# Seven steps instead of one ahead of a group of transposes, their copies on VectorE, and an output block in other PSUM banks

## The chip, the cores and the metric

The kernel runs on one core of a Trainium2 chip. The metric is the device time of one launch in microseconds (us). TensorE (PE in the profile) multiplies matrices out of SBUF into the banks of PSUM; VectorE (DVE), ScalarE (ACT) and GpSimd (POOL) work on SBUF and PSUM; SyncE (SP) issues the transfers. Each engine runs its own instructions in order and waits on semaphores for the others. A difference of 0.2% is 3.05 us here.

## The reference, cut to what matters

One layer of a diffusion backbone: 1024 latent and 256 context tokens of width 1024, all in fp32. One input projection feeds two groups of heads, a gated DeltaNet in chunks of 64 tokens and a neighbourhood attention; one output projection takes both back to the residual stream.

```python
def gated_deltanet(p, ...):                # p = modulate(rms_norm(x)) @ w_in
    qkv = short_conv(p[..., :3 * DN_WIDTH], conv_w)
    ...
    q = l2_normalize(q) * DN_HEAD_DIM ** -0.5
    k = l2_normalize(k)
    ...
def chunk_gated_delta_rule(q, k, v, g, beta, S0):
    m = jnp.where(strict, einsum("bhncd,bhnmd->bhncm", kb, k) * decay, 0.0)
    a_mat = jnp.eye(CHUNK) + m
    u = triangular_solve(a_mat, v * beta, lower=True, unit_diagonal=True)
    w = triangular_solve(a_mat, kb * exp(gam), lower=True, unit_diagonal=True)
    ...
x = x + g1 * (concatenate([dn_x, na_x], axis=-1) @ w_out)      # the output projection
x = x + g2 * swiglu(modulate(rms_norm(x, norm2_w), sh2, sc2), w_ffn_in, w_ffn_out)
```

The kernel solves the triangular systems by inverses: it inverts 32x32 diagonal blocks of `a_mat` and builds the rest of each chunk's inverse from them by matmuls.

## The kernel before, in words

**Matmuls.** A product of fp32 accuracy is made of three: each operand is split into a high part and a rest (`whi`, `wlo` of the weights, `hh`, `hl` of the activations) and PE sums `hh`*`whi`, `hl`*`whi` and `hh`*`wlo`. For each block of 128 weight columns SP loads `wraw` (line 216), ACT casts it to `whi` (217), and POOL or DVE makes `wlo` (219). `wraw`, `whi` and `wlo` have two buffers each.

**The projection stage.** `jobs` is a list of blocks of output columns. A Block of 1024 tokens is 48 matmuls: 8 steps of the contraction, k, with 3 products into 2 PSUM banks (`blk`). The order that matters here is `nk3` (a wide one of 1280 tokens), `nq0`, `nq1`, `nq2`, `q0`, `q1`, `q2`, `q3`. After a block ACT takes its banks out (line 463, `cacc<-blk`); one block later its norm is made: PE sums squares with matmuls `m<-cr,cst` and `pr<-cr,cst`, ACT reads those banks (line 521), DVE scales (528, 534) and so on. The banks named `m` are two, and are shared by everything that asks for a small bank: the norms and the transposes below.

**Work between the matmuls.** Two generators, `block_inverses()` and then `preps()`, are queued as background work `bg`. After each step k of a block the loop does `bg.step(1)` (for blocks ahead of `turn`, thus up to `q0`), which runs the generator to its next `yield`; what it emits there lands at this place of every engine's program. So a `yield` moves everything that follows in the two generators by one step k, six matmuls.

**block_inverses().** `N` holds the 80 groups of 32x32 blocks, one group a partition. DVE eliminates over the columns (lines 914 and 916, from wide to narrow). Then comes a memset of the diagonal (919), and 8 PE transposes each into two `m` banks (`m<-cst,N`, line 925), copied out of each bank to `WK` (927; `U` is a view of `WK`), with a yield after every second bank: four groups of 8 transposes. Then DVE transposes in squares (933), scales (936), and SP stores the halves to `x_d` (935, 938). Line 103 and line 99 of the profile are the helpers through which all transposes and matmuls go.

**preps().** It loads `xc` from `x_d` (965), `kk` and `e`, spreads `xc` into `fx` and `y` (977, 978), multiplies `kk` by `e` on DVE (982), and then PE makes `pr<-fx,kk` and three `pr<-y,kk`, with copies between them (992, 1000). It is done four times before it needs the queries' blocks, up to `q1`.

**The output projection.** Eight blocks b of 128 output channels, 48 matmuls each for b = 2 to 5, into two banks. ACT and DVE take the products out: `add` is one `scalar_tensor_tensor` into `x2` per bank (line 1460), a square on ACT (1465) and an addition to `acc` (1474) on DVE. Blocks 0 and 1 were begun earlier in other banks (`sc`). The scans before had a PSUM pool `psg`, whose tag `ps` has two banks; `scopes.close()` gives it back and the pool `psf` (8 banks) is opened, ahead of block 2. Between, DVE also works on `acc` from `wad` (lines 251 and 253) for the second half of the modulation.

The order of instructions of each engine is that of the program's text, so it is fixed when the kernel is built.

Of the kernel before, what the change touches and what calls it, by code (L numbers as in the profile page):

```python
# [16 lines left out]
PSUM = bass.MemoryType.PSUM  # L17
# [71 lines left out]
def hybrid(ctx, tc, a, dbg):  # L89
    nc = tc.nc  # L90
    act, dve, pool, sp = nc.scalar, nc.vector, nc.gpsimd, nc.sync
# [16 lines left out]
    def pools(stack, name, side=None, bufs=1, **kw):  # L108
        if side:
            kw["side"] = side  # L110
        return stack.enter_context(tc.tile_pool(name=name, bufs=bufs, reuse_waits="tile", **kw))
# [111 lines left out]
    def modulation(adp, qs, bank):  # L223

        order = [(q, k) for q in qs for k in range(KT)]
        landing = []

        def fetch():
            if order:
                q, k = order.pop(0)  # L230
                x = adp.tile([128, 512], F32, name="wad", tag="wad", bufs=4)
                sp.dma_start(x, a["wa2"][q, :, k])
                landing.append(x)

        def reduce(q, acc2):
            p = bank()
            for b in range(4):
                pe.matmul(p[:, b:b + 1], acc2[:, b * 128:(b + 1) * 128], ones[:, 0:1], start=True, stop=True)
            s = slice(16 + q * 4, 20 + q * 4)
            dve.tensor_tensor(modp[:, s], p[:, 0:4], bada[:, s], OP.add)  # L240

        for _ in range(3):
            fetch()
        prev = None
        for q in qs:
            acc2 = adp.tile([128, 512], F32, name="acc2", tag="acc2", bufs=2)
            for k in range(KT):
                yield
                x, sc = landing.pop(0), sc2[:, k, 0:1]
                if k == 0:  # L250
                    dve.tensor_scalar(acc2, x, sc, None, op0=OP.mult)
                else:
                    dve.scalar_tensor_tensor(acc2, x, sc, acc2, op0=OP.mult, op1=OP.add)  # L253
                fetch()
                if k == 7 and prev is not None:
                    reduce(q - 1, prev)
            prev = acc2
        for _ in range(6):
            yield
        reduce(qs[-1], prev)  # L260
# [133 lines left out]
    with ExitStack() as bs:  # L394
# [7 lines left out]
        def bank(name="m"):  # L402

            if len(psum) == 1:
                return psum[0].tile([128, 512], F32, name=name, tag="ps")
            return psum[1].tile([128, 512], F32, name=name, tag=name, bufs=4 if name == "blk" else 2)
# [235 lines left out]
        with ExitStack() as xs:  # L642
# [93 lines left out]
            ps = [bank() for _ in SEGS]  # L736
# [117 lines left out]
        def block_inverses():  # L854
            with ExitStack() as gs:
# [4 lines left out]
                P = 2 * NU  # L860
                fl = lambda x: x.rearrange("p u i -> p (u i)")
                with ExitStack() as g3s:
# [18 lines left out]
                    for i, (d, u0, n) in enumerate(cuts):  # L881
                        rcs, nxt = nxt, rhs(*cuts[i + 1]) if i + 1 < len(cuts) else None
                        p = bank()
# [17 lines left out]
                    for i0 in range(0, 32, 4):  # L901
                        p = bank()
# [14 lines left out]
                    yield  # L917
                flat = N.rearrange("p b r c -> p b (r c)")
                dve.memset(flat[:P, :, 0:1024:33], 1.0)
                yield  # L920
                U = WK.rearrange("p d u i -> p (d u) i")
                for i0 in range(0, 32, 4):
                    p = bank()
                    for i in range(4):
                        pe.transpose(p[:, i * P:(i + 1) * P], N[:P, :, :, i0 + i].rearrange("p b r -> p (b r)"),
                                     ident[:P, :P])
                    act.copy(U[:, :, i0:i0 + 4], p[:, :4 * P].rearrange("p (i u) -> p u i", i=4))
                    if i0 % 8 == 4:
                        yield
                for d in range(2):  # L930
# [144 lines left out]
        for n in range(2, len(jobs) + 2):  # L1075
            j = jobs[n] if n < len(jobs) else None
            if n == inv:
                bg2.drain()
                bg2s.close()
                early.close()  # L1080
                psum.append(bs.enter_context(tc.tile_pool(name="psa", bufs=1, space=PSUM)))
                bg.add(block_inverses())
                bg.add(preps())
# [71 lines left out]
    scopes = ExitStack()  # L1155

    with ExitStack() as gs:
# [4 lines left out]
        ps = scopes.enter_context(tc.tile_pool(name="psg", bufs=1, space=PSUM))  # L1162
# [282 lines left out]
    def normed(t):  # L1445

        s, p = HV[t], bank()
        pe.matmul(p, ones, acc[:, s], start=True, stop=True)
        act.activation(rs[:, s], p, AF.Ln, bias=b_eps, scale=1.0 / D)
        act.activation(rs[:, s], rs[:, s], AF.Exp, scale=-0.5)  # L1450

    with ExitStack() as os_:
        ws = [load_w(a["w_out"][b, :, :4], kt=4, lo_engine=dve) for b in range(2)]
        late = Background()
        late.add(modulation(pools(os_, "adp", "left"), range(4, 6), bank))

        held = tc.keep_in_program_order

        def add_x(b, s, p):
            return dve.scalar_tensor_tensor(x2[:, b, s], p, modp[:, 16 + b:17 + b], x2[:, b, s],  # L1460
                                            op0=OP.mult, op1=OP.add)

        def square(b, s):
            sq = uw.tile([128, 4, 128], F32, name="ws", tag="ws", bufs=3).rearrange("p a b -> p (a b)")
            act.activation(sq, x2[:, b, s], AF.Square)
            return sq

        def add(b, s, p):

            add_x(b, s, p)  # L1470
            if b == 0:
                act.activation(acc[:, s], x2[:, b, s], AF.Square)
                return
            dve.tensor_tensor(acc[:, s], acc[:, s], square(b, s), OP.add)

        for b in range(2):
            sp.dma_start(x2[:, b], a["xcT"][b, :, CT:])
        for b, (w, outs) in enumerate(zip(ws, begun)):
            for k in range(4):
                for j, (wi, xi) in enumerate(((0, 0), (0, 1), (1, 0))):  # L1480
                    for o, s in zip(outs, HV):
                        pe.matmul(o, w[wi][:, k], parts[xi][k][:, s], start=False, stop=k == 3 and j == 2,
                                  skip_group_check=True)
                if b and k % 2:
                    late.step()
            for p, s in zip(outs, HV):
                add(b, s, p)
            sp.dma_start(x2_d[b], x2[:, b])
            if b == 0:
                nxt = load_w(a["w_out"][2], lo_engine=dve)  # L1490
                up = Stream()
        scopes.close()
        ps = pools(ctx, "psf", bufs=8, space=PSUM)
        for b in range(2, KT - 2):
            w, nxt = nxt, load_w(a["w_out"][b + 1], lo_engine=dve)
            sp.dma_start(x2[:, b], a["xcT"][b, :, CT:])
            outs = [bank(), bank()]
            for k in range(KT):
                for j, (wi, xi) in enumerate(((0, 0), (0, 1), (1, 0))):
                    for o, s in zip(outs, HV):  # L1500
                        pe.matmul(o, w[wi][:, k], parts[xi][k][:, s], start=k == 0 and j == 0,
                                  stop=k == KT - 1 and j == 2)
                if k % 2:
                    late.step()
            for p, s in zip(outs, HV):
                add(b, s, p)
            sp.dma_start(x2_d[b], x2[:, b])
            if b >= KT - 4:
                up.make()
                up.make()  # L1510
        late.drain()
        dve.scalar_tensor_tensor(w2s, modp[:, 32:40], 1.0, n2w, op0=OP.add, op1=OP.mult)
        ws = [nxt, load_w(a["w_out"][KT - 1], lo_engine=dve)]
        for b in (KT - 2, KT - 1):
            sp.dma_start(x2[:, b], a["xcT"][b, :, CT:])
        last = []
        for t, s in enumerate(HV):
            outs = [bank(), bank()]
            last.append(outs)
            for k in range(KT):  # L1520
                for j, (wi, xi) in enumerate(((0, 0), (0, 1), (1, 0))):
                    for o, w in zip(outs, ws):
                        pe.matmul(o, w[wi][:, k], parts[xi][k][:, s], start=k == 0 and j == 0,
                                  stop=k == KT - 1 and j == 2)
                    if t == 1 and k == 2 and j == 0:
                        normed(0)
            if t == 0:
                for _ in finish(0):
                    pass
                up.make()  # L1530
                up.make()
# [294 lines left out]
```

## Time and profile before

| | |
|---|---|
| median of 3 runs | 1525.72 us (1524.1 to 1526.36) |
| profiled execution | 1523.36 us, span 1521.6 us |
| PE busy | 1460.3 us, 96% of the span |
| DVE busy | 1004.2 us, 66% |
| ACT busy | 709.5 us, 47% |
| POOL busy | 184.5 us, 12% |
| granted TensorE clock, mean | 0.992 |

All durations below come from the profiled execution; what lies outside of its span is 1.8 us. Times at the start of a row count from the span's start. The number in brackets behind a row is the time for which the engine was idle before it, with what ended it. A row that stands for x2 or more instructions of one shape spans all of them; rows of PE overlap a little, since matmuls are pipelined.

### The profile page before, as it was taken

The numbers are of one execution on the slowest core, as the hardware profiler recorded it, in microseconds if no ns is written. First come the engines' busy times: TensorE is split into PE (matmuls) and PEld (weight loads), VectorE is DVE, ScalarE is ACT, GpSimd is POOL, SyncE is SP. The second block draws the span as 40 slices with busy tenths as digits, with TensorE's granted clock in tenths as the row PEclk, the third lists the DMA queues.
The fourth block names the chain that finished last, engine by engine and source line by source line (L and its number), as shares of the span: only waits on it lengthen the run. The fifth ranks groups of instructions, "written<-read, shape, count | busy, mean of one in ns | idle before, by whom it ended". The sixth has DMA issues, their size and how long they took to land.

```text
span 1521.6 us, 23480 instructions
## 1 busy us (share of the span) xinstructions
PE 1460.3 (96%) x8365; PEld 1206.3 (79%) x8365; DVE 1004.2 (66%) x1898; ACT 709.5 (47%) x1387; POOL 184.5 (12%) x253
## 2 busy tenths in 40 slices
PE   6999998999999999998899999999999999999998
PEld 3789787778877778887787888788888888888887
DVE  4887579354687327779976398755565556699652
ACT  5443362683376546566643284333333334354441
POOL 0154610342135300000100000000000000000000
PEclk9999999899999999999999999999999999999999
DMA  9377223654477799997529405333333335798742
GB/s 366 114 232 235 61 79 124 232 148 168 134 225 251 220 287 275 281 287 226 164 81 314 147 35 181 118 105 104 104 105 102 104 104 172 253 367 287 236 152 83
DMA packets 209829, 276.28 MB, mean 182 GB/s; under 512 B 15968, under 2 KB 116912, under 8 KB 208688
## 3 DMA queue, kind: packets, MB, share of 16 engines
q1 hardware_dynamic: 208992, 274.41, 56.0%
q8 instruction: 66, 1.08, 0.3%
q10 hardware_dynamic: 720, 0.37, 0.1%
q14 instruction: 51, 0.42, 0.1%
HBM read 209.93 MB, written 68.98 MB: 183 GB/s over the span
## 4 chain that ended last, share of the span: by engine, by line
PE 70%; DVE 14%; DMA 5%; issue 4%; ACT 4%; POOL 1%; SPq 0%; POOLq 0%; DVEq 0%; ACTq 0%
PE ps L99 45%; PE blk L99 12%; PE sc L99 5%; PE m L99 3%; PE pr L99 2%; PE sc L103 2%; DVE tt L914 2%; DVE N L916 2%; DVE cacc L472 1%; DMA wad<-wa 1%; DVE acc L253 1%; PE m L103 1%; PE pm L99 1%; ACT bt L341 1%; DVE bt L338 1%
## 5 line engine op out<-in xcount | busy, mean ns | idle before, releaser
L99 PE MATMUL ps<-hT,uhi 128*128 128x512 f32 x496 | 146.8, 390 | 1.5 <-DVE e L1701 1.4
L99 PE MATMUL ps<-lT,uhi 128*128 128x512 f32 x496 | 146.4, 390 | 0.0
L99 PE MATMUL ps<-hT,ulo 128*128 128x512 f32 x496 | 146.2, 389 | 0.0
L99 PE MATMUL blk<-hh,whi 128*128 128x512 f32 (+1 forms) x456 | 138.9, 396 | 2.0 <-ACT hh L715 1.3
L99 PE MATMUL blk<-hh,wlo 128*128 128x512 f32 (+1 forms) x456 | 129.1, 377 | 0.0
L99 PE MATMUL ps<-hB,uhi 128*128 128x512 f32 x436 | 129.1, 390 | 0.0
L99 PE MATMUL ps<-lB,uhi 128*128 128x512 f32 x436 | 128.9, 389 | 0.0
L99 PE MATMUL ps<-hB,ulo 128*128 128x512 f32 x436 | 128.7, 389 | 0.0
L99 PE MATMUL blk<-hl,whi 128*128 128x512 f32 (+1 forms) x456 | 128.6, 376 | 0.0
L1411 ACT CAST uhi<-ws 128x512 fp32r<-128x512 f32 x91 | 54.7, 622 | 144.8 <-PE ps L99 77.5
L1411 ACT CAST uhi<-wq 128x512 fp32r<-128x512 f32 x101 | 60.3, 620 | 131.0 <-PE ps L99 67.3
L1412 DVE TENSOR_TENSOR ulo<-wq,uhi 128x512 fp32r<-128x512 f32 x101 | 67.2, 688 | 65.0 <-ACT uhi L1411 35.6
L99 PEld LDWEIGHTS ps<-hT,uhi 128*128 128x128 f32 x496 | 93.0, 188 | 21.3 <-ACT uhi L1411 1.8
L99 PEld LDWEIGHTS ps<-lT,uhi 128*128 128x128 f32 x496 | 93.0, 188 | 19.7 <-DVE lT L1564 0.4
L99 PEld LDWEIGHTS ps<-hT,ulo 128*128 128x128 f32 x496 | 93.1, 188 | 19.4
L99 PEld LDWEIGHTS ps<-hB,uhi 128*128 128x128 f32 x436 | 81.9, 188 | 17.4 <-issue 0.5
L99 PEld LDWEIGHTS ps<-lB,uhi 128*128 128x128 f32 x436 | 81.8, 188 | 17.3 <-DVE lB L1564 0.3
L99 PEld LDWEIGHTS ps<-hB,ulo 128*128 128x128 f32 x436 | 81.9, 188 | 17.0
L99 PEld LDWEIGHTS blk<-hh,wlo 128*128 128x128 f32 x456 | 80.6, 190 | 17.7 <-issue 2.5
L99 PEld LDWEIGHTS blk<-hl,whi 128*128 128x128 f32 x456 | 81.0, 190 | 15.7
L99 PEld LDWEIGHTS blk<-hh,whi 128*128 128x128 f32 x456 | 77.2, 192 | 18.8 <-ACT hh L715 3.2
L338 DVE CUSTOM_DVE_ANT_0 bt<-sc,bt 128x640 f32<-128x640 f32 x64 | 52.5, 822 | 49.1 <-issue 38.3
(335 smaller groups left out, 3061.0 us busy)
## 6 DMA issues: line engine op xcount, KB each, us to landing
wq<-w_fo SPq DMA_DIRECT2D x99, 256.0 KB
wq<-w_gu SPq DMA_DIRECT2D x88, 256.0 KB
wad<-wa SPq DMA_DIRECT2D x64, 256.0 KB
bt<-rpb SPq DMA_DIRECT2D x64, 192.0 KB
t_d<-g SPq DMA_DIRECT2D x22, 512.0 KB
fr<-t_d SPq DMA_DIRECT2D x44, 256.0 KB
f_d<-g SPq DMA_DIRECT2D x33, 256.0 KB
fr<-f_d SPq DMA_DIRECT2D x33, 256.0 KB
```

The source lines that it names most:

```text
L99: i = nc.tensor.matmul(*args, **kw)
L103: i = nc.tensor.transpose(*args, **kw)
L253: dve.scalar_tensor_tensor(acc2, x, sc, acc2, op0=OP.mult, op1=OP.add)
L338: dve.tensor_tensor_reduce(bt, sc[:, u * 640:u * 640 + 640], bt, 1.0, -3.0e38, OP.add, OP.max, m[:, 0:1])
L341: act.activation(bt, bt, AF.Exp, bias=m[:, 1:2], accum_out=m[:, 2:3])
L472: dve.scalar_tensor_tensor(acc[:, d0:d1], p[:, d0 + o - s0:d1 + o - s0], cw[:, blk, tap:tap + 1], acc[:, d0:d1], op0=OP.mult, op1=OP.add)
L914: dve.tensor_tensor(t, N[:P, :, 0:c, c:c + 1].to_broadcast([P, 4, c, w]), N[:P, :, c:c + 1, c + 1:32].to_broadcast([P, 4, c, w]), OP.mult)
L916: dve.tensor_tensor(N[:P, :, 0:c, c + 1:32], N[:P, :, 0:c, c + 1:32], t, OP.add)
L1411: act.copy(hi, self.raw[key])
L1412: dve.tensor_tensor(lo, self.raw[key], hi.bitcast(F32), OP.subtract)
```

## The change

Three edits. First, in `block_inverses()` six more yields stand between the memset of the diagonal and the transposes. Second, the copies out of the transposes' banks are DVE's instead of ACT's. Third, block 2 of the output projection takes its two banks from the scans' pool, which is closed at block 3. Lines from 920 on move by one, lines from 1495 on by two.

```diff
@@ -917,14 +917,15 @@
                 flat = N.rearrange("p b r c -> p b (r c)")
                 dve.memset(flat[:P, :, 0:1024:33], 1.0)
-                yield
+                for _ in range(7):
+                    yield
                 U = WK.rearrange("p d u i -> p (d u) i")
                 for i0 in range(0, 32, 4):
                     p = bank()
                     for i in range(4):
                         pe.transpose(p[:, i * P:(i + 1) * P], N[:P, :, :, i0 + i].rearrange("p b r -> p (b r)"),
                                      ident[:P, :P])
-                    act.copy(U[:, :, i0:i0 + 4], p[:, :4 * P].rearrange("p (i u) -> p u i", i=4))
+                    dve.tensor_copy(U[:, :, i0:i0 + 4], p[:, :4 * P].rearrange("p (i u) -> p u i", i=4))
                     if i0 % 8 == 4:
                         yield
@@ -1489,9 +1490,10 @@
-        scopes.close()
-        ps = pools(ctx, "psf", bufs=8, space=PSUM)
         for b in range(2, KT - 2):
+            if b == 3:
+                scopes.close()
+                ps = pools(ctx, "psf", bufs=8, space=PSUM)
             w, nxt = nxt, load_w(a["w_out"][b + 1], lo_engine=dve)
             sp.dma_start(x2[:, b], a["xcT"][b, :, CT:])
             outs = [bank(), bank()]
```

PE around the transposes. Before, all 32 stand in the second half of `nq0`, four k steps of it; the numbers behind `m` and `blk` tell the buffers apart, and what an instruction waits for stands in brackets. The first group and the second:

```order
L99 MATMUL blk_2349<-hh4_414,whi_2225 128x512
L103 MATMUL m_2364<-cst_71,N_1544 128x80 [waits DVE_49]
...
L103 MATMUL m_2370<-cst_71,N_1544 128x80 x4
L99 MATMUL blk_2349<-hh4_414,wlo_2226 128x512
L103 MATMUL m_2382<-cst_71,N_1544 128x80 [waits Activation_49]
L103 MATMUL m_2382<-cst_71,N_1544 128x80 x3
L103 MATMUL m_2388<-cst_71,N_1544 128x80 [waits Activation_49]
```

After it, on the same engine, the first group stands behind the last matmul of `nq0`, then comes the norm of `nk3` (`cr_2341`), then step 0 of `nq1` and the second group (the third and fourth stand behind its steps 1 and 2):

```order
L103 MATMUL m_2400<-cst_71,N_1544 128x80 [waits DVE_49]
...
L103 MATMUL m_2406<-cst_71,N_1544 128x80 x4
L99 MATMUL pr_2421<-cr_2341,cst_71 128x512 [waits Activation_49]
L99 MATMUL m_2415<-cr_2341,cst_71 128x256 [waits DVE_49]
L99 MATMUL m_2418<-cr_2341,cst_71 128x512 [waits DVE_49]
L99 MATMUL blk_2441<-hh0_133,whi_2344 128x512
...
L99 MATMUL blk_2442<-hh0_133,wlo_2345 128x512
L103 MATMUL m_2449<-cst_71,N_1544 128x80 [waits Activation_49]
L103 MATMUL m_2449<-cst_71,N_1544 128x80 x3
L103 MATMUL m_2455<-cst_71,N_1544 128x80 [waits Activation_49]
```

The two `m` banks now go from the first group to the norm of `nk3` and from there to the second group, which waits for ACT's reading of `m_2415` and `m_2418`. ACT's program at this place after the change (before it, the eight copies of line 927 stood ahead of the first of these rows; `whi_2436` is the weights of `nq2`, `blk_2349` the banks of `nq0`):

```order
L217 CAST whi_2436<-wraw_2435 128x1024 [waits DMAHW1_49,PE_49,Pool_49]
L463 ACTIVATE cacc_2412<-blk_2349 128x512 [waits DVE_49,PE_49]
L463 ACTIVATE cacc_2412<-blk_2350 128x512 [waits PE_49]
L521 ACT_TABLE_LOAD
L521 ACTIVATE cr_2341<-pr_2421,bias_62 128x512 [waits PE_49]
L521 ACTIVATE cr_2341<-m_2415,bias_62 128x256 [waits PE_49]
L504 ACTIVATE cr_2433<-cacc_2412 128x1024 [waits Activation_49]
L521 ACTIVATE cr_2341<-m_2418,bias_62 128x512 [waits PE_49]
```

ACT reads the two banks behind the cast of the weights and the emptying of `nq0`'s banks. In the output projection PE's program keeps its order, but the waits move. Before, block 2 (`ps_8277`, `ps_8278`) and the start of block 3 (`ps_8355`):

```order
L99 MATMUL ps_8277<-gah_4925,whi_8202 128x512 [waits Activation_49]
L99 MATMUL ps_8278<-gah_4925,whi_8202 128x512 [waits DVE_49]
...
L99 MATMUL ps_8355<-gah_4925,whi_8271 128x512 [waits Activation_49]
```

After, block 2 is `ps_8273` and `ps_8274`, and block 3 begins with `ps_8355` again:

```order
L99 MATMUL ps_8273<-gah_4925,whi_8202 128x512 [waits Activation_49]
L99 MATMUL ps_8274<-gah_4925,whi_8202 128x512 [waits PE_49]
...
L99 MATMUL ps_8355<-gah_4925,whi_8267 128x512 [waits DVE_49,Activation_49]
```

The wait for DVE has moved from the second matmul of block 2 to the first of block 3. What that one waits for on DVE is the second of these two additions of block 2, which stand on DVE behind the making of block 3's `wlo` (`wlo_8268`):

```order
L219 TENSOR_TENSOR wlo_8268<-wraw_8266,whi_8267 128x1024 [waits DMAHW4_49,Activation_49]
L1461 SCALAR_TENSOR_TENSOR x2_8149<-ps_8273,modp_63,x2_8149 128x512 [waits DMAHW5_49,PE_49]
L253 SCALAR_TENSOR_TENSOR acc2_8241<-wad_8288,sc2_104,acc2_8241 128x512 [waits DMAHW6_49,DVE_49]
L1461 SCALAR_TENSOR_TENSOR x2_8149<-ps_8274,modp_63,x2_8149 128x512 [waits PE_49]
```

From the end of `q1` on, the engines' programs hold the same instructions in the same order, apart from a few rows of DVE and SP in blocks 2 to 4 of the output projection.

## The prediction

> **What bounds the kernel now.** I read the page's busy times first, then PE's rows with their waits and the stretches around the two places of the change, then from the waits back to ACT, DVE and the transfers.
>
> ```profile
> PE 1460.3 (96%) x8365; PEld 1206.3 (79%) x8365; DVE 1004.2 (66%) x1898; ACT 709.5 (47%) x1387; POOL 184.5 (12%) x253
> ```
>
> PE is busy 96% of the span: a change pays only by what it takes from PE's idle time, or from time at half clock. PE's rows at the first place (`nq0` up to 277.38, the norm of `nk3`, `nq1` to 290.47, its norm, the first prep):
>
> ```profile
> 259.76 0.39 PE L99 MATMUL blk<-hh,whi 128*128 128x512 f32 x1
> 265.52 0.53 PE L103 MATMUL m<-cst,N 80*128 80x80 f32 x2 [5.37 <-DVE N L919]
> 277.38 1.45 PE L99 MATMUL m<-cr,cst 128*128 128x256 f32 x4
> 279.13 1.03 PE L99 MATMUL blk<-hh,whi 128*128 128x512 f32 x2
> 294.90 2.02 PE L99 MATMUL pr<-fx,kk 128*128 128x96 f32 x8 [2.55 <-DVE kk L982]
> 308.18 1.10 PE L99 MATMUL pr<-fx,kk 128*128 128x96 f32 x8 [0.49 <-DVE kk L982]
> ```
>
> The brackets are what the change aims at: 5.37 us until DVE has finished `N`, then waits for `kk`. The stretches (PE busy, then the clock, third from last) show what follows a stall:
>
> ```profile
> 260.00:265.50 5.50, 0.15 (x1) 0.00 (x0) 5.16 (x11) 0.00 (x0) 0.00 (x0) 0.87 0.26 103
> 265.50:270.00 4.50, 4.48 (x21) 3.90 (x22) 0.75 (x3) 1.46 (x4) 0.00 (x0) 0.50 0.45 157
> 270.00:274.00 4.00, 4.00 (x21) 3.57 (x20) 0.58 (x1) 1.95 (x5) 0.00 (x0) 0.50 0.40 143
> 294.90:301.00 6.10, 6.10 (x39) 4.94 (x39) 0.93 (x2) 4.98 (x11) 3.08 (x9) 0.73 0.92 292
> ```
>
> After the 5.37 us PE works at half clock until 274: busy, but worth half, so (4.48 + 4.00) x 0.50 = 4.2 us are lost, 4.4 with the tail behind 274. After the 2.55 us wait 6.10 x 0.27 = 1.65 are lost. At this place before loses 5.37 + 4.4 + 2.55 + 1.65 + 0.49 = 14.5 us.
>
> **First edit: seven steps.** PE does the remaining 24 matmuls of `nq0` without stopping. A block of 48 at full clock takes 10.9 us (first row below), 0.227 each, so `nq0` ends at 259.76 + 24 x 0.227 = 265.2. DVE's elimination is not sped up:
>
> ```profile
> 821.20:832.10 10.90, 10.90 (x50) 9.03 (x49) 7.17 (x11) 2.33 (x4) 0.00 (x0) 1.00 0.76 236
> 265.30 0.17 DVE L919 MEMSET N<- 80x128 f32 x1
> 266.04 0.28 DVE L916 TENSOR_TENSOR N<-N,tt 80x120 f32<-80x120 f32 x1
> ```
>
> The first two transposes wait for the memset (265.47), the others for the last addition (266.32), and the norm behind them for DVE's copies of their banks (about 0.3): 1.4 us of idle in place of 5.37. The norm takes 279.13 - 277.38 = 1.75, step 0 of `nq1` 6 x 0.227; PE is at the second group of transposes at about 270.1.
>
> Here a new wait begins. The second group needs the two `m` banks, and they come free when ACT has read the norm of `nk3`. ACT does its program in order, and ahead of these reads stands the cast of `nq2`'s weights:
>
> ```profile
> 277.60 1.04 ACT L217 CAST whi<-wraw 128x1024 fp32r<-128x1024 f32 x1 [4.20 <-PE blk L99]
> 278.55 1.08 ACT L463 ACTIVATE cacc<-blk 128x512 f32<-128x512 f32 x2
> 279.64 1.28 ACT L521 ACT_TABLE_LOAD   x1
> 280.94 1.06 ACT L521 ACTIVATE cr<-m,bias 128x256 f32<-128x256 f32 x2
> 281.88 0.70 ACT L521 ACTIVATE cr<-pr,bias 128x512 f32<-128x512 f32 x1
> 282.45 1.07 ACT L504 ACTIVATE cr<-cacc 128x1024 f32<-128x1024 f32 x1
> ```
>
> What releases the cast decides the case. The row names PE (the end of `nq0`, 277.38, frees the buffer of `whi`), which would come 12 us earlier after the change. But the cast also needs its weights in SBUF, and the transfer rows show these late:
>
> ```profile
> 251.65 11.60 SPq L1059 DMA_DIRECT2D vw_d<-nv_d x6
> 263.34 4.38 SPq L216 DMA_DIRECT2D wraw<-w_nqk x1
> DMA packets 239, 0.62 MB, mean 159 GB/s; under 512 B 4, under 2 KB 4, under 8 KB 238
> DMA packets 69, 0.05 MB, mean 104 GB/s; under 512 B 3, under 2 KB 65, under 8 KB 69
> DMA packets 23, 0.12 MB, mean 393 GB/s; under 512 B 0, under 2 KB 0, under 8 KB 23
> ```
>
> The load is issued behind copies from DRAM to DRAM. Its packets are 512 B; the three transfer rows are for 271 to 274.9 (nearly none of them: the big copies hold the queue), 276.5 to 277 (still 65) and 277.3 to 277.6 (none). So the weights land at about 277.3 whatever PE does, and the cast starts near 277.6 as before. Behind it: `blk` (1.0), table (1.3), then at 280.94 `pr` (about 0.6), `m` of 256 (about 0.45). The first bank is free at 282.05, so PE stands for 282.05 - 270.1 = 12.0 us. The second bank comes 1.07 (line 504) and 0.6 later; PE has four transposes to do in it, so 1.0 more. [...] I take 2.5, with the ends 1.65 and 4.4.
>
> **The preps behind it.** The copies, squares and stores slide. DVE makes the last scaling of the norm (first row below, to 290.5) when it did before, since ACT's work up to it is the same in sum; the last two copies follow it. Then, by the other rows:
>
> ```profile
> 289.01 1.49 DVE L534 TENSOR_TENSOR hl<-cacc,hl 128x1280 f16<-128x1280 f32 x1 [1.32 <-ACT hl L533]
> 280.65 1.51 DVE L933 STREAM_TRANSPOSE ut<-WK 128x1280 f32<-128x1280 f32 x1 [4.19 <-DMA x_d<-ut]
> 282.27 1.49 DVE L936 TENSOR_TENSOR WK<-WK,NB 128x1280 f32<-128x1280 f32 x1
> 283.79 0.32 SPq L938 DMA_DIRECT2D x_d<-WK x1
> ```
>
> Square and scale 3.0, the wait for the store 4.2, square and scale 3.1: the last store goes at 291.5 + 10.3 = 301.8, 18.0 later than its 283.79. The first `pr` started 11.1 behind that store (294.90), so now at 312.9. PE gets there at 282.05 + 1.0 + 1.6 (24 transposes) + 42 x 0.227 + 2.5 + `nq2` 10.9 + two norms of 1.4 = 310.4, and waits 2.5 (0 to 4, since both ends have errors of a microsecond or two). What is late next is nothing on PE: four preps of some 3 us then go into `q0` and `q1` as they went into `nq2` and `q0`. Sum for this edit: 1.4 + 12.0 + 1.0 + 2.5 + 2.5 = 19.4 against 14.5, so **+4.9**. Ends: +2 (no prep wait, short half clock), +9 (long half clock, prep wait 4).
>
> [...]
>
> **Second edit: copies on DVE.** ACT's took 0.425 each, which is the first row; DVE's of nearby shapes (the other rows) 0.42 for 256 and 0.55 for 384 elements a partition, so about 0.48 for 320.
>
> ```profile
> L927 ACT COPY WK<-m 128x320 f32<-128x320 f32 x8 | 3.4, 425 | 12.7 <-PE m L103 12.2
> L1000 DVE COPY y<-pr 32x384 f32<-32x384 f32 x4 | 2.2, 554 | 3.6 <-PE pr L99 3.6
> L1000 DVE COPY y<-pr 32x256 f32<-32x256 f32 x4 | 1.7, 420 | 4.9 <-PE pr L99 4.8
> ```
>
> Eight copies are 3.8 us of DVE work; DVE waits for PE between them, so they cost PE only the 0.3 above. On ACT they would stand behind the late cast too, so this edit avoids a worse wait and brings no gain of its own.
>
> **Third edit: block 2 in the scans' banks.** Before:
>
> ```profile
> 803.62 0.39 PE L99 MATMUL ps<-gah,whi 128*128 128x512 f32 x1
> 807.68 0.80 PE L99 MATMUL ps<-gah,whi 128*128 128x512 f32 x1 [3.67 <-DVE x L1460]
> 807.70:813.40 5.70, 5.70 (x14) 4.45 (x15) 4.29 (x7) 0.59 (x1) 0.00 (x0) 0.50 0.96 318
> 814.27 1.05 ACT L217 CAST whi<-wraw 128x1024 fp32r<-128x1024 f32 x1 [5.98 <-DMA wraw<-w_out]
> 815.35 1.23 DVE L219 TENSOR_TENSOR wlo<-wraw,whi 128x1024 fp32r<-128x1024 f32 x1 [3.29 <-ACT whi L217]
> ```
>
> Block 2 runs from 803.62 to 821.20, 17.6 against 10.9: 3.67 of wait (and a little around it) and 5.70 x 0.50 = 2.85 at half clock. After the change block 2 does not wait and ends at 814.5. Block 3's first matmul then waits for DVE's second addition of block 2. DVE gets to it behind `wlo` of block 3, whose cast waits for its weights until 814.27: 816.5, an addition (0.7), one of line 253 (0.75), the second addition (0.7), about 818.6. A stall of 4.1, then half clock as before, about 2.6: the 6.7 us are spent one block later. I take 0, from -1 to +1.
>
> **The sum.** +4.9 and 0: the execution like the profiled one (1523.36) goes to 1528.3; the median of the runs is 2.36 above it, so 1525.72 + 4.9 = **1530.6**. A difference below 3.05 us (0.2%) can't be told from none.
>
> **Rivals.**
> 1. *The weights land in time, faster.* If the load of `wraw` isn't held by the copies (they keep 271 to 274.9 full now), the cast goes at 266, ACT reads the banks by 270.5, and the second group hardly waits: 5.37 + 4.4 give way to 1.4, so -8.4 at the first edit, 1517.3. It decides at a cast before about 266. The cast's row names PE, which speaks for it; the transfer rows speak against it. Chance 0.10.
> 2. *The output block's wait goes.* If DVE came to block 2's additions at once at 814.5, block 3 would wait 1.5 and keep the clock: -5.2 there, -0.3 in all, 1525.4. It needs the cast of block 3's weights before 812. The 5.98 us wait of that cast for its transfer speaks against it. Chance 0.13.
> 3. *The preps come later still.* DVE's second scaling of the inverses falls at about 299 to 302, where POOL makes the next `wlo`. These two rows show what a meeting costs:
>
> ```profile
> 254.84 2.92 POOL L219 TENSOR_TENSOR wlo<-wraw,whi 128x1024 fp32r<-128x1024 f32 x1 [44.56 <-ACT whi L217]
> 255.51 2.95 DVE L914 TENSOR_TENSOR tt<-N 80x672 f32<-80x672 f32 x1
> 258.50 0.85 DVE L916 TENSOR_TENSOR N<-N,tt 80x672 f32<-80x672 f32 x1
> ```
>
> The same shape took 2.95 beside POOL and 0.85 alone, 2.1 more. With that and 1.65 of half clock behind a prep wait of 4.6 the sum is +8.7, 1534.4. It decides if `wlo` starts before DVE's scaling. Chance 0.15. [...]
>
> **How the numbers follow.** The forecast has 0.60 (its own range 1528 to 1533), the rivals 0.10, 0.13 and 0.15; 0.02 is left for something else. The range 1523.5 to 1536 leaves out the first rival and little more. Slower by over 0.2%: 0.60 + 0.15, less the 0.05 of the forecast that falls below +3.05, 0.70. Same: the second rival and that 0.05, 0.18. Faster: 0.12.
>
> **What would show it.** In the changed kernel's PE rows: no idle of 5 us before 265; about 12 us of idle near 270 to 282, released by ACT's line 521; a clock of 0.5 behind it; the first `pr` near 313 after a wait; no idle at 804 and one of about 4 us one block later, before block 3, with 0.5 behind it. The forecast is wrong if ACT's cast of the weights starts well ahead of 277, or if block 3 starts without a wait.

## The result, and the profile after

The change made the kernel slower: 1532.53 us median of 5 runs (1531.66 to 1538.46) against 1525.19 (1522.06 to 1526.36), a ratio of 1.0054, 95% interval 1.0038 to 1.0071, so 7.3 us more on the medians. The forecast was 1530.6, slower. The profiled executions differ by 15.1 us (spans 1536.7 and 1521.6), 7.8 more than the medians: that of after, at 1538.46, was the slowest of its five and 5.9 above their median, and that of before, at 1523.36, was 1.8 below its own. Where these lie is shown below.

PE's rows with their waits at the transposes, after (those of before stand in the prediction):

```profile
265.57 0.45 PE L103 MATMUL m<-cst,N 80*128 80x80 f32 x2
266.43 0.90 PE L103 MATMUL m<-cst,N 80*128 80x80 f32 x6 [0.41 <-DVE N L916]
282.31 0.80 PE L103 MATMUL m<-cst,N 80*128 80x80 f32 x4 [11.40 <-ACT cr L521]
283.83 0.80 PE L103 MATMUL m<-cst,N 80*128 80x80 f32 x4 [0.72 <-ACT cr L521]
313.61 1.13 PE L99 MATMUL pr<-fx,kk 128*128 128x96 f32 x8 [1.46 <-DVE kk L983]
316.85 0.41 PE L99 MATMUL pr<-y,kk 128*32 128x32 f32 x8 [1.15 <-ACT kk L993]
345.19 0.44 PE L99 MATMUL pr<-y,kk 128*32 128x32 f32 x8 [1.83 <-ACT kk L993]
```

The 5.37 us wait for `N` is gone. In its place stands one of 11.40 us ahead of the second group of transposes, released by ACT's line 521, and behind the preps two waits for ACT's line 993 that before did not have. What ACT did around those 11 us:

```profile
256.09 1.28 ACT L504 ACTIVATE cr<-cacc 128x1280 f32<-128x1280 f32 x1
277.86 1.04 ACT L217 CAST whi<-wraw 128x1024 fp32r<-128x1024 f32 x1 [20.50 <-DMA wraw<-w_nqk]
278.81 1.07 ACT L463 ACTIVATE cacc<-blk 128x512 f32<-128x512 f32 x2
279.91 1.28 ACT L521 ACT_TABLE_LOAD   x1
281.20 0.69 ACT L521 ACTIVATE cr<-pr,bias 128x512 f32<-128x512 f32 x1
281.79 0.47 ACT L521 ACTIVATE cr<-m,bias 128x256 f32<-128x256 f32 x1
```

ACT stood for 20.50 us before the cast of `nq2`'s weights, and now the row names the transfer: the cast started at 277.86, 0.26 later than before. The clock behind the wait, by stretches (behind the stretch and its length stand the busy times of PE, its weight loads, DVE, ACT and POOL; the clock is third from last):

```profile
274.00:280.00 6.00, 0.00 (x0) 0.00 (x0) 0.00 (x0) 2.12 (x4) 1.01 (x1) 0.59 0.14 48
280.00:285.00 5.00, 1.97 (x10) 1.64 (x11) 0.82 (x2) 4.97 (x6) 1.33 (x1) 0.50 0.37 108
285.00:290.00 5.00, 5.00 (x22) 4.10 (x21) 3.34 (x5) 2.60 (x3) 0.00 (x0) 0.62 0.00 2
345.00:350.00 5.00, 4.81 (x26) 3.53 (x27) 4.00 (x6) 4.01 (x9) 2.27 (x3) 0.68 0.80 208
```

1.97 x 0.50 + 5.00 x 0.38 = 2.9 us are lost at half clock there, and 4.81 x 0.32 = 1.5 behind the last wait of the preps. The output blocks, after:

```profile
833.52 0.70 PE L99 MATMUL ps<-gah,whi 128*128 128x512 f32 x2 [3.81 <-DVE x L1461]
833.50:838.50 5.00, 4.97 (x15) 3.99 (x16) 4.29 (x6) 1.65 (x2) 0.00 (x0) 0.66 0.92 282
```

Block 2 has no wait, block 3 one of 3.81 us with half clock behind it (4.97 x 0.34 = 1.7).

**Where the time went.** PE's matmuls are as many in both traces, so the start of the same matmul can be compared. From one in `nk3` (248.8 us) to one behind `q1` (353.0 us of before) after loses 9.0 us; from there to the scans' end (777) another 6.1; over the output blocks (777 to 845) it gains 1.0; from there to the last matmul it loses 0.6. The first is the place of edits one and two. The 6.1 us lie where the programs hold the same instructions: 1.3 of them up to 525, where edit three alone (below) loses 1.7, and 4.8 in the start of the attention (525 to 620). Before's stretch and after's, with the same work in them:

```profile
560.00:564.00 4.00, 4.00 (x47) 3.81 (x45) 3.31 (x12) 2.76 (x6) 0.31 (x1) 1.00 0.88 284
```

```profile
570.00:574.00 4.00, 2.87 (x16) 2.73 (x17) 1.74 (x6) 4.00 (x16) 0.31 (x1) 0.76 0.49 149
574.00:578.00 4.00, 4.00 (x40) 3.83 (x39) 3.10 (x12) 1.32 (x3) 0.31 (x1) 0.81 0.58 194
```

In these two stretches 4.00 x 0.24 + 4.00 x 0.19 = 1.7 us are lost at a lower clock. Ahead of them PE also idled longer than before: two waits, of 1.26 and 1.86, stand where before has one of 1.34.

```profile
567.08 2.19 PE L99 MATMUL ps<-vk,kt 128*128 128x128 f32 x16 [1.26 <-ACT vk L1209]
571.13 0.77 PE L103 MATMUL sc<-cst,bt 128*128 128x128 f32 x5 [1.86 <-DVE bt L343]
```

PE waits first for ACT's `vk`, and ACT stood for 5.30 us ahead of that, against 3.11 in before. The row of after names a matmul; but that of before names the end of a store, and so does that of the run with edits one and two alone (the second row, from its trace), which has the same loss:

```profile
553.43 2.17 ACT L1208 ACTIVATE vk<-ps,KB 128x128 f32<-128x128 f32 x8 [3.11 <-DMA zT_d<-zt]
566.07 2.18 ACT L1209 ACTIVATE vk<-ps,KB 128x128 f32<-128x128 f32 x8 [5.00 <-DMA zT_d<-zt]
```

By these rows a store that ended some 2 us later stands at the head of this part; why it did is not shown. The part does not belong to the edits: edit one alone, with `q1` just as late, has ACT's wait at 3.09 and loses 0.7 from 525 to 620. Of after's five runs the two at 1536.75 and 1538.46 us had a mean clock of 0.987 and 0.988, the three at 1531.66 to 1532.53 one of 0.990 and 0.991. So the median's 7.3 us are near 9.0 less 1.0; that the three faster runs lack the other losses fits their clock, but they have no trace.

### The profile page after: what moved, and what is told of

It reads as the page before. It is cut to its first block, busy times and chain, and to the rows that moved or that the text cites. A ratio compares the mean times of both kernels' runs of the same rounds, so it can differ in the third digit from the quotient of the medians.

```text
span 1536.7 us, 23479 instructions
## 1 busy us (share of the span) xinstructions
PE 1463.0 (95%) x8365; PEld 1208.3 (79%) x8365; DVE 1011.3 (66%) x1906; ACT 708.9 (46%) x1381; POOL 187.8 (12%) x253
## 4 chain that ended last, share of the span: by engine, by line
PE 70%; DMA 9%; DVE 9%; ACT 6%; issue 3%; POOL 1%; SPq 1%; ACTq 0%; POOLq 0%; DVEq 0%
PE ps L99 44%; PE blk L99 15%; PE sc L99 4%; PE pr L99 2%; DMA nv_d<-zt 2%; PE m L99 2%; PE sc L103 2%; DMA wad<-wa 1%; DMA wraw<-w_nqk 1%; DMA bt<-rpb 1%; DVE acc L253 1%; DMA xt<-xcT 1%; PE m L103 1%; DMA xc<-x_d 1%; ACT bt L341 1%
## 5 line engine op out<-in xcount | busy, mean ns | idle before, releaser
L99 PEld LDWEIGHTS ps<-hT,uhi 128*128 128x128 f32 x496 | 93.0, 188 | 21.9 <-issue 2.8
```

Source lines behind the costliest of these rows:

```text
L99: i = nc.tensor.matmul(*args, **kw)
```

## The experiments

T is the theory of the prediction: the second group of transposes is held by ACT, which in order waits for late weights. For each run I give its time against before in runs beside it on the same chip, and, from its trace, the change over two stretches against the profiled execution of before: A, from the matmul in `nk3` to the one behind `q1`, and C, over the output blocks. The change itself has A +9.0, C -1.0.

**Edits one and two without three.**

```diff
 (after, with these lines as before)
+        scopes.close()
+        ps = pools(ctx, "psf", bufs=8, space=PSUM)
         for b in range(2, KT - 2):
-            if b == 3:
-                scopes.close()
-                ps = pools(ctx, "psf", bufs=8, space=PSUM)
```

> Edits one and two alone (seven steps, copies on VectorE); the output block stays as before. Theory T (the loss comes from the second group of transposes, held behind ScalarE's cast of nq2's weights, which land at about 277, and from what slides with it): PE idle of 11 to 12.5 us near 270 to 282, q1 ends 8 to 10 us later than before, and a time 6 to 10 us above before; the wait of 3.7 us in block 2 stays. Rival U (the third edit is what costs): q1's end no more than 2 us later, time within 2 us of before.

1534.31 against 1526.77, ratio 1.0053 (1.0032 to 1.0075). A +8.5, C -0.9, with block 2 as before; PE waited 11.27 us for line 521. So these two edits make the whole loss, as T has it (8 to 10 at `q1`, 6 to 10 in time), and a C of -0.9 comes without edit three, so the change's own -1.0 is not shown to be its work.

**Edit three alone.**

> Edit three alone. Theory T (the wait of block 2 moves to block 3, since the new pool's first bank is block 2's second): block 2 without a wait, about 3.5 to 4.2 us of idle before block 3 and half clock behind it, time within 1.5 us of before. Rival U (edit three costs): 5 to 8 us slower. Rival V (edit three takes the wait away and the loss elsewhere hides it): 4 to 7 us faster.

1526.43 against 1526.77, ratio 0.9998 (0.9979 to 1.0018); C -0.2. Block 3 waits:

```profile
819.83 1.19 PE L99 MATMUL ps<-gah,whi 128*128 128x512 f32 x2 [3.90 <-DVE x L1460]
```

As T had it: the wait moves and nothing is gained.

**Edit three with a bank passed over.**

```diff
             if b == 3:
                 scopes.close()
                 ps = pools(ctx, "psf", bufs=8, space=PSUM)
+                dve.memset(bank()[:1, :1], 0.0)
```

> Edit three with one bank of the new pool passed over (a one-element memset on VectorE uses it up), so that block 3 gets banks 7 and 6 instead of 0 and 7. Theory T: the only thing that holds block 3 is the bank, so it then waits only for its own weights (cast from 814.27 to 815.3, the low part to 816.5, against an end of block 2 at 814.5): 1 to 2 us of idle, full clock, 4 to 6 us faster than before. Rival W (VectorE's lateness, not the bank, is what block 3 waits for): as with edit three alone, within 1.5 us of before.

1520.59 against 1526.77, ratio 0.9958 (0.9942 to 0.9973): 6.2 us faster; C -5.3. The stretches over the start of blocks 2 and 3:

```profile
805.00:810.00 5.00, 5.00 (x24) 4.14 (x23) 4.83 (x8) 4.11 (x8) 0.00 (x0) 1.00 1.04 392
815.00:820.00 5.00, 4.19 (x17) 2.85 (x17) 2.83 (x5) 1.68 (x2) 0.00 (x0) 1.00 1.00 338
```

0.81 us of idle are left, while block 3's weights are cast, and the clock stays at 1.00. In the built program block 2 has PSUM banks 1 and 0 (those of the scans), and the new pool gives out 0, 7, 6 and so on; block 3 began with 0, which DVE had still to read. W, that DVE's lateness would hold it anyway, falls: block 3 starts at 817.31, while DVE begins the second addition of block 2 only at 819.76.

**The copies from DRAM to DRAM later, so that the weights come early.**

```diff
-                    copies.step(2)
+                    if n >= later:
+                        copies.step(2)
```

> Edits one and two, and the sixteen copies from DRAM to DRAM are issued some five blocks later (during the v blocks), so that nq2's weights land early. Theory T: ScalarE's cast starts when nq0 ends, near 265.5, the idle of 11 to 12 us ahead of the second group shrinks to 1 or 2 us without half clock behind it; the preps then still wait some 4 to 5 us for the stores, so q1 ends 0 to 4 us earlier than before and the time is 8 to 13 us below that of edits one and two alone. Rival X (the transposes' later place itself costs, by the preps that meet other work, whatever the weights do): still 3 us or more slower than before.

1535.15 against 1526.77, ratio 1.0058 (1.0035 to 1.0080); A +10.3. This one told nothing: SyncE's rows show the copies and the load as they were.

```profile
253.07 11.60 SPq L1060 DMA_DIRECT2D vw_d<-nv_d  x6
264.77 4.38 SPq L216 DMA_DIRECT2D wraw<-w_nqk  x1
```

The built program has them where they were (the load at 264.77, behind the six copies): the text's order is not always the engine's, and the description at the start is too simple there. In the next runs the copies are kept in their place by `tc.keep_in_program_order`.

> Edits one and two with the sixteen copies from DRAM to DRAM held in program order behind the q blocks, so that SyncE's program really has nq2's weights ahead of all of them (in the run before, the build had put the copies back to where they were). Theory T (ScalarE's late cast holds the banks): weights in SBUF by 265, the cast at 265.5 to 266, idle ahead of the second group of transposes at most 2 us in place of 11.4, no half clock there; the preps then wait for their stores 3 to 5 us, so q1 ends between 5 us earlier and 1 us later than before, that is 8 to 14 us earlier than with edits one and two alone. Rival X (the transposes' place itself costs): q1 still ends 6 us or more later than before.

A -7.0: against the change's +9.0 the same two edits end `q1` 16 us earlier, 2 more than the best that T gave. ACT and PE:

```profile
266.94 1.05 ACT L217 CAST whi<-wraw 128x1024 fp32r<-128x1024 f32 x1 [7.67 <-PE blk L99]
270.87 0.47 ACT L521 ACTIVATE cr<-m,bias 128x256 f32<-128x256 f32 x1
272.64 1.01 PE L103 MATMUL m<-cst,N 80*128 80x80 f32 x8
```

The cast waits for nothing but `nq0`, the second group has no wait, and the clock stays at 1.00 from 254 to 316. X falls. But the time was 1536.32 against 1526.89, ratio 1.0066 (1.0043 to 1.0088), since the copies now stand ahead of another load, whose cast ACT again waits for ahead of the emptying of the banks (line 478) that PE needs:

```profile
371.51 16.02 SPq L1060 DMA_DIRECT2D vw_d<-nv_d  x6
387.63 2.37 SPq L216 DMA_DIRECT2D wraw<-w_conv  x1
400.25 1.04 ACT L217 CAST whi<-wraw 128x1024 fp32r<-128x1024 f32 x1 [14.90 <-DMA wraw<-w_conv]
401.62 0.80 PE L99 MATMUL blk<-hh,whi 128*128 128x512 f32 x1 [12.44 <-ACT cr L478]
```

**Control: the copies moved, edits one and two not made.**

> The kernel before with only the sixteen copies moved behind the q blocks. Control for the run above. Theory T: the wait of 5.4 us for VectorE's elimination and the half clock behind it stay, q1 ends within 2 us of before, time within 3 us of before. If the copies' place matters by itself, q1 ends 3 us or more away from before.

1540.55 against 1526.89, ratio 1.0089 (1.0071 to 1.0106). A -1.4, and the same 12.44 us wait at 407.93. So the copies' place gives 1.4 of the 7.0, and the rest of that gain is the edits', once the weights are early. On the time I expected within 3 us of before and was wrong (+13.7): I had not followed what the copies would meet at their new place.

**Edit one alone**, with ACT's copies.

> Edit one alone: seven steps, the copies stay on ScalarE. There the first two copies stand behind the late cast too. Theory T: PE stops one stage earlier, at the norm of nk3 (near 268 until 279), and q1 ends 8 to 12 us later than before: as late as with edits one and two, or up to 2 us later. Rival Y (VectorE's copies are what costs): q1 ends within 3 us of before.

1534.53 against 1526.89, ratio 1.0057 (1.0037 to 1.0077); A +9.0.

```profile
278.86 2.93 PE L99 MATMUL m<-cr,cst 128*128 128x256 f32 x4 [10.88 <-ACT WK L928]
```

PE stops one stage earlier, for the same cast, and loses the same. Y falls for the change as a whole.

**Edit two alone.**

> Edit two alone: one step, the copies on VectorE (0.47 to 0.50 us each instead of 0.425). Theory T: no effect to speak of, the 5.4 us wait stays, q1 ends within 1 us of before and the time is within 2 us of before. Rival Y (VectorE's copies cost or gain): q1 ends 2 us or more away.

1528.99 against 1526.89, ratio 1.0021 (1.0005 to 1.0036); A +2.8. The expectation of no effect was wrong. The copies took 0.49 each, but the build put DVE's second scaling behind the norm's:

```profile
286.32 1.55 DVE L528 SCALAR_TENSOR_TENSOR cacc<-cacc,qkw,cr 128x1280 f32<-128x1280 f32 x1 [3.31 <-ACT cr L525]
287.79 1.49 DVE L936 TENSOR_TENSOR WK<-WK,NB 128x1280 f32<-128x1280 f32 x1
301.00 2.02 PE L99 MATMUL pr<-fx,kk 128*128 128x96 f32 x8 [6.17 <-DVE kk L982]
```

The last store goes 6 us later (289.80 against 283.79), and PE's first prep waits 6.17 in place of 2.55. By these rows it is the order on DVE that cost, not the copies' 0.07 each; no run holds that order apart.

**Towards a version that gains from both places.** In three runs the copies stand singly in the v blocks (`if n >= later and k % 2 == 0: copies.step(1)`, in program order): with edits one and two, with all edits and the bank passed over, and with the bank passed over but without edits one and two.

> Edits one and two with the copies from DRAM to DRAM spread one by one over the v blocks, in program order, so that no load of weights stands behind more than a few of them. Theory T: as in the run with the copies held behind the q blocks, q1 ends about 7 us earlier than before counted from the start of nq0 (5.4 of wait and 4.4 of half clock go, 3 come back as waits of the preps); the 13 us wait for weights that run had near 390 does not come, so this stays: 4 to 9 us faster than before. Rival Z (the copies cost some 10 us wherever they stand): a wait of PE for weights or stores of 5 us or more in the v blocks, time as before or slower.

> The same, with edit three and one bank passed over (block 3 in banks 7 and 6). Theory T: both gains add: 7 at the transposes and 5 at the output block, 9 to 14 us faster than before, about 1515. Rival Z: no faster than the run with the passed-over bank alone (about 6 us below before).

> The same without edits one and two: one step, copies on ScalarE, the copies from DRAM to DRAM spread, one bank passed over. Theory T: the wait for the elimination and its half clock stay; 4 to 7 us faster than before from the output block, and 5 to 8 us slower than the run above. If the copies' place were what gains, as fast as the run above.

| run | time, before beside it | ratio (95%) | A | C |
|---|---|---|---|---|
| edits 1 and 2, copies spread | 1534.26, 1526.60 | 1.0058 (1.0038 to 1.0077) | -4.3 | -0.3 |
| all edits, copies spread, bank passed over | 1529.59, 1526.60 | 1.0022 (1.0009 to 1.0035) | -4.9 | -6.1 |
| edit 3, copies spread, bank passed over | 1534.72, 1526.60 | 1.0068 (1.0048 to 1.0087) | -0.5 | -5.3 |

C came as T has it, and A in the forecast's direction but less than its 7; the times did not (4 to 9 and 9 to 14 us faster were expected, and 4 to 7). Only the gap between the last two rows, 5.1, is in T's 5 to 8. Z came true in a form I had not named: the weights of the last `z` block came late in all three runs. SyncE's last load of them in before, and then, in the run with all edits, that load, its cast and PE:

```profile
514.67 0.55 SPq L216 DMA_DIRECT2D wraw<-w_z  x1
```

```profile
534.88 0.56 SPq L216 DMA_DIRECT2D wraw<-w_z  x1
541.95 1.04 ACT L217 CAST whi<-wraw 128x1024 fp32r<-128x1024 f32 x1 [3.73 <-DMA wraw<-w_z]
543.05 1.22 PE L99 MATMUL blk<-hh,whi 128*128 128x512 f32 x2 [5.78 <-ACT whi L217]
```

From 525 to 560 each of the three loses 14 to 16 us. SyncE issued that load behind the attention's first loads and not ahead of them. With the copies kept together (the run of A -7.0) it stands ahead of them, at 524.52 against 533.33, and that run loses 1.5 there; that spreading the copies led the build to the other order is inferred from this and from the three runs.

**The cast on GpSimd, no transfer moved.** All edits, the bank passed over, and for `nq2` alone another engine's copy is handed to the helper that loads and casts (its new argument is left out here):

```diff
-                jobs[n + 1].prefetch()
+                jobs[n + 1].prefetch(**({"cast": pool.tensor_copy} if n == inv + 6 else {}))
```

> All three edits, one bank passed over ahead of block 3, and the cast of nq2's weights alone moved from ScalarE to GpSimd (which then makes the low part as before). No transfer is moved, and the weights still land near 277. Theory T (what holds the second group of transposes is only that ScalarE, in order, waits for these weights): ScalarE reads the norm's banks by 272, the idle of 11.4 us ahead of the second group goes, no half clock there; nq2 starts without a wait if GpSimd has cast by 283; q1 ends 4 to 7 us earlier than before (as in the three runs with the copies moved), the output block gives 5 more, and nothing is lost later since SyncE's program hardly changes: 8 to 13 us faster than before, about 1516. Rival (the gain needs the weights early, whoever casts them): PE waits 5 us or more at the start of nq2, and the time is no better than with the passed-over bank alone (6 us faster).

1519.75 against 1526.37, ratio 0.9960 (0.9946 to 0.9974); A +0.8, C -6.0.

```profile
280.40 2.55 SPq L546 DMA_DIRECT2D nk_d<-hl  x4
283.67 0.41 SPq L939 DMA_DIRECT2D x_d<-ut  x1
276.17 1.04 POOL L217 CAST whi<-wraw 128x1024 fp32r<-128x1024 f32 x1 [20.25 <-DMA wraw<-w_nqk]
268.87 1.01 PE L103 MATMUL m<-cst,N 80*128 80x80 f32 x8
289.35 1.51 DVE L934 STREAM_TRANSPOSE ut<-WK 128x1280 f32<-128x1280 f32 x1 [8.31 <-DMA x_d<-ut]
301.41 2.02 PE L99 MATMUL pr<-fx,kk 128*128 128x96 f32 x8 [5.65 <-DVE kk L983]
301.40:308.00 6.60, 6.59 (x35) 4.84 (x35) 0.98 (x2) 4.44 (x16) 3.82 (x10) 0.57 0.90 274
```

The weights land nearly as late as in the change (GpSimd's cast waits for them until 276.17, in a trace that is 1.8 us ahead of before's from the start), yet the second group, at 268.87, has no wait: what held it is ACT's turn, not the weights as such. `nq2` starts without a wait too, so the rival falls in its mechanism. But T's time (8 to 13 us faster) and its `q1` (4 to 7 earlier) did not come; the gain is lost by the first prep, some 30 us later: DVE waits 8.31 us for the store of the first scaled half (SyncE issued it at 283.67, behind four stores of the norm), PE 5.65 for the preps, and 6.59 x 0.43 = 2.8 go at half clock. GpSimd's subtraction, which now follows its cast (277.29 to 279.69), also met DVE's first scaling there, which took 2.90 in place of 1.49. So the chain inverses, store, load, prep is the next bound. The 6.6 us are those of the passed-over bank, which alone does as well (0.9958); no version here is clearly faster than that one. (The start names GpSimd among the engines that work on SBUF and PSUM; its instructions in the kernel before and in this run read and write SBUF alone.)

## Why the prediction was right

Edits one and two, forecast +4.9, were +9.0 in the trace of after and +8.5 in that without edit three; edit three, forecast 0, was -0.2 alone. The main mechanism is right: the wait, what releases it, and its size. That the sum came near the median is partly luck: 9.0 is the upper end of the forecast's +2 to +9, which was given for a long half clock and a prep wait of 4, and neither came. By its steps:

- *The weights land late whatever PE does.* Right: the cast started at 277.86 (277.6). Early weights and another engine for the cast each took the wait away.
- *The wait of 12.0, the bank's 1.0, the first 1.4, half clock 2.5.* 11.40, 0.72, 0.56 (the 0.41, and 0.15 between the end of `nq0` at 264.81 + 0.61 and 265.57) and 2.9: 15.6 against 16.9. (The pieces up to the first free bank make 281.99, not 282.05; PE went on at 282.31.) No run shows what sets the length of the half clock: the 2.5 was my estimate between the 1.65 and the 4.4 that before lost behind its waits of 2.55 and 5.37, and what was measured is 2.9 behind the 11.40, and 2.8 behind the 5.65 of the run with GpSimd's cast.
- *The prep wait of 2.5.* 1.46, and the clock stayed at 1.00 behind it (313.61 to 320); that the sum had no half clock there was my estimate. The step behind it is the one that failed: "What is late next is nothing on PE". PE waited 1.15 and 1.83 more for ACT's copies of `kk` (line 993), 0.38 at one more row, and lost 1.5 at half clock behind the last: 4.9 us with no term in the sum. ACT had the norms of `nq1` and `nq2`, casts and the preps together in `q0` and `q1`. From 340 to 345 it was busy for 4.99 of 5.00 us, and the copy for which PE waited until 345.19 stood last (a short row of 341.98 is left out):

```profile
340.94 1.14 ACT L523 ACTIVATE cr<-cr,bias 128x1024 f32<-128x1024 f32 x1
342.17 1.57 ACT L982 ACTIVATE e<-e,GN 128x128 f32<-128x128 f32 x5
343.65 1.12 ACT L540 CAST hl<-cacc 128x512 f16<-128x512 f32 x2
344.68 0.46 ACT L993 COPY kk<-pr 128x384 f32<-128x384 f32 x1
```

The listed losses of after come to 21.9 us against before's 14.5; of the 9.0 the remaining 1.6 lie in rows without a wait and are not resolved.
- *Rival 3's meeting.* It happened: DVE's second scaling took 2.95 beside POOL's `wlo`, the first 1.49 alone.

```profile
298.52 2.39 POOL L219 TENSOR_TENSOR wlo<-wraw,whi 128x1024 fp32r<-128x1024 f32 x1 [17.19 <-ACT whi L217]
299.31 2.95 DVE L937 TENSOR_TENSOR WK<-WK,NB 128x1280 f32<-128x1280 f32 x1
```

It did not show as a longer first wait, since PE came to the first `pr` at 312.1 and not at 310.4. Its sum of +8.7 was nearer than the forecast's +4.9, though by other terms. What the rows show is the time, 2.95 against 1.49; why the two engines meet is not shown.
- *Edit two costs nothing.* True inside the change (A +9.0 with it, and +9.0 with edit one alone), not by itself (+2.8).
- *The wait of block 2 moves to block 3.* Right, 3.81 for 4.1, with 1.7 at half clock for 2.6. The second rival, that the wait goes, needed another bank, and with it gave -5.3, where the forecast had -5.2 for DVE coming early.

## What to carry to other kernels

A yield that moves work past another user of the same two buffers can make it wait for that user's reader: before moving it, follow the buffers, and on the reader's engine everything ahead of the reading, up to the slowest transfer. A wait that moves with a pool can be one bank, as here (6.2 us faster with it passed over); look at which bank comes first and who read it last. Of a stall that is taken away, ask what chain ends next: here three cures took the 11 us wait away, and the time went to a load of weights, to another, and to the preps.

## What was not expected of the hardware

In the run with its cast GpSimd cast 128x1024 elements in 1.04 us by the profile, as fast as ACT in the change (1.04), while its subtraction of the same size took 2.40. And in the start of the attention, where by ACT's rows a store ended some 2 us later, stand two waits of 1.26 and 1.86 where before has one of 1.34, and behind them stretches at 0.76 and 0.81 of the clock: together 4.8 us in two traces, and 0.7 in a third with the same instructions there.
